# 64x64 array quarters instead of block-diagonal 128x128 operands in the recurrence of block 1

## The chip, the cores and the metric

The kernel runs on one core of a Trainium2 chip. The metric is the device time of one execution in microseconds (us), as a median of several runs; the profile is one further execution, with its own span. The core has a matrix engine (TensorE: PE for its matmuls, PEld for its weight loads), three engines that work on vectors (VectorE: DVE, ScalarE: ACT, GpSimd: POOL) and queues that start DMA transfers (SP is the one that loads weights). Each engine works through its own instructions in order and waits on semaphores for the others.

## What is computed

A chain of layers for 256 tokens of width 1024. Block 1 is an RWKV7 layer with its output projection, a dense feed-forward, an attention layer and a mixture of experts; block 2 is two further transformer layers with a context sequence. Only the RWKV7 recurrence is touched by the change. For each of 16 heads of 64 channels it carries a 64x64 state S over the tokens (wkv7_scan of the reference):

```python
def step(S, inp):
    r_t, w_t, k_t, v_t, a_t, b_t = inp
    sa = jnp.einsum('bhvk,bhk->bhv', S, a_t)
    S = (S * w_t[:, :, None, :] + sa[..., None] * b_t[:, :, None, :]
         + v_t[..., None] * k_t[:, :, None, :])
    return S, jnp.einsum('bhvk,bhk->bhv', S, r_t)
...
y = wkv7_scan(_heads(r), _heads(decay), _heads(k), _heads(v), -kk, kk * a_h)
```

All of it is float32. The rest of the layer, and all else in the program, is the same in both kernels.

## The kernel before

The function wkv does the recurrence in chunks of 64 tokens: four chunks for the 256 tokens, and two heads (a pair, 128 channels) at a time, so that there are eight pairs. Within a chunk the recurrence becomes matrix products of 64x64 blocks and the inverse of a triangular 64x64 matrix. A pair goes through four stages, each a Python generator that yields after each step:

- prep (8 steps): decays, the scaled vectors b and k and the queries, then the pairwise products g1 and g2 within each chunk, masked by VectorE into Aab, Rb, Aak, Rk, and b and k turned token-major (Btok, Ktok).
- invert (17 steps): (I - A)^-1 by merging diagonal blocks from 2 to 64 in five levels. In each level Q is transposed into T, X = mask * (Aab T), Q = Q + X Q.
- walk (14 steps): the four chunks one after another, since each needs the state S of the one before.
- finish (3 steps): group norm, bonus, gate, and the split of the result yT for the output projection.

The two heads of a pair stand side by side on the 128 partitions. To keep them apart in one 128x128 product, the operands are **block-diagonal**: each chunk has 128 columns, of which one 64x64 block belongs to each head and the other two are zero. The buffers bbd, kbd, abd and rbd are zeroed once by GpSimd and only their diagonal blocks are written; the masks have zeros off the blocks. So a tile for one pair is 128x512, a step of invert is four matmuls of 128x128 (function blocks) or four transposes (function transposes), and VectorE masks or adds 128x512 elements.

All products of the recurrence are float32 matmuls. In the trace each stands as two records on PE, each with its own weight load on PEld, and we call such a record a pass; a transpose is one pass.

At most a few pairs are in flight. The list stages gives each stage a start and a length in units of a pair's turn, and the steps of all pairs are sorted by that due time; each engine's instructions then stand about in that order. So prep of one pair, invert of an earlier one and walk of a still earlier one alternate on the engines. Behind every sixth step of wkv (ADA_EVERY = 6) comes one step of another job, ada, which computes block 2's modulation: it loads 1 MB of ada_w (two 512 KB tiles of the six-tile pool wraw, two tiles of which the gate weights hold meanwhile) and does four matmuls with 32 stationary columns and 512 moving columns. These four go to four column groups of the array (written 128*32 in the trace). There are 48 such steps; their DMAs are the only large loads during wkv.

The tiles of the recurrence lie in slots that the projections have left and in five tiles of the pool whl (the names wkvd and wkvx in the rows). When the last pair's result is there, the output projection rwkv_out begins (whi,yTh in the rows).

Of the kernel before, what the change touches and what calls it, by code (L numbers as in the profile page):

```python
# [16 lines left out]
P = 128  # L17
T = 256
# [21 lines left out]
# weight groups held for the last token tile; weights loaded before the lent tiles come in; transposed pairs whose  # L40
# scaling VectorE shares; columns per piece of a weight's split
# [17 lines left out]
def shape_consts():  # L59
    """Masks, permutations and rotary tables: they depend on shapes alone."""  # L60
# [14 lines left out]
    add("bd_strict", same64 & (r < c))  # L75
    add("bd_incl", same64 & (r <= c))
    add("lv0T", ((r // 2) == (c // 2)) & (r < c))
    for lv in range(1, 6):
        b = 2 ** lv
        add(f"lv{lv}", ((r // (2 * b)) == (c // (2 * b))) & ((r // b) % 2 == 1) & ((c // b) % 2 == 0))  # L80
# [39 lines left out]
    groups = {"consts_w": ("bd_strict", "bd_incl", "lv0T", "lv1", "lv2", "lv3", "lv4", "lv5"),  # L120
# [16 lines left out]
def pack(inputs):  # L137
    """Only layout: every vector that goes along partitions is laid out as [128, n]."""
# [20 lines left out]
class Wt:  # L159
    """A weight unit on chip: k-tiles of [128, ncol], as high and low parts."""  # L160
# [16 lines left out]
class Act:  # L177
    """Activations with the contraction on partitions: k-tiles of [128, ntok], high and low parts."""
# [5 lines left out]
class Net:  # L184
    def __init__(self, ctx, tc, a):
# [12 lines left out]
        # tiles that the next weights are loaded into (None: one of their own)  # L198
# [80 lines left out]
    def split(self, hi, lo, src):  # L279
        """src as hi + lo, both readable by the fast float32 matmul."""  # L280
# [3 lines left out]
    def rpow(self, out, x, n, mul, add):  # L284
        """out = (x * mul + add) ** -0.5 for an [128, n] tile."""
# [5 lines left out]
    def wload(self, src, nk, ncol):  # L291
        """Loads [nk*128, ncol] by parts of at most 1024 columns of k-tiles and splits them."""
# [66 lines left out]
    def mmT(self, out, w, x, nk, w0, w1):  # L359
        """out [w1 - w0, 256] = w^T x over nk k-tiles, the weights being the stationary operand."""  # L360
# [6 lines left out]
    def lin_T(self, ch, x, nk, src, n, evac, mcol=P):  # L367
        """Channel-major output: for units of 256 columns evac(c0, ntiles, psum [128, ntiles, 256])."""
# [17 lines left out]
    def to_T(self, ch, src, x, nk=KD, scale=None, bias=None, f32=None):  # L386
        """src(tb) token-major [128, nk*128] -> x (channel-major hi/lo), optionally scaled and shifted per channel."""
# [34 lines left out]
    def layer_norm(self, h, gi, out):  # L422
        """In: h[tb] pre-norm sums [128,1024]; out(tb) normalised, ln_g/ln_b row gi = (layer, which)."""
# [74 lines left out]
    # LoRA hidden states, channel-major: tanh(xw @ w1), xa @ a1, sigmoid(xg @ g1)  # L498
# [42 lines left out]
    # kk = normalised k * k_k per head  # L541
# [36 lines left out]
def wkv(N, st, ch=0):  # L578
# [43 lines left out]
    for x in ("bbd", "kbd", "abd", "rbd"):  # L622
        for t in bufs[x]:
            nc.gpsimd.memset(t, 0.0)
# [1431 lines left out]
```

## Time and profile before

| | |
|---|---|
| median of 3 runs | 2950.31 us (2949.16 to 2954.93) |
| span of the profiled execution | 2942.9 us |
| PE busy | 2824.4 us (96%) |
| PEld busy | 2336.0 us (79%) |
| DVE busy | 2279.5 us (77%) |
| ACT busy | 1809.3 us (61%) |
| mean granted TensorE clock | 0.976 |

The runs' times are 6 to 12 us above the span: they hold what lies around the program's own instructions. In the rows, PE is busy while a matmul is somewhere in the array; matmuls overlap in it, so the busy time of a group is more than its share of the engine, and the time of a steady stream is read from the starts of its records. 128*64 behind the tiles' names is the part of the array that a matmul takes: rows (contraction) times columns (stationary columns). "x8" counts records. The clock is given as a share of full speed, 1.0 for 2.4 GHz and 0.5 for 1.2 GHz.

### The profile page before, as it was taken

The numbers are of one execution on the slowest core, as the hardware profiler recorded it, in microseconds if no ns is written. First come the engines' busy times: TensorE is split into PE (matmuls) and PEld (weight loads), VectorE is DVE, ScalarE is ACT, GpSimd is POOL, SyncE is SP. The second block draws the span as 40 slices with busy tenths as digits, with TensorE's granted clock in tenths as the row PEclk, the third lists the DMA queues.
The fourth block names the chain that finished last, engine by engine and source line by source line (L and its number), as shares of the span: only waits on it lengthen the run. The fifth ranks groups of instructions, "written<-read, shape, count | busy, mean of one in ns | idle before, by whom it ended". The sixth has DMA issues, their size and how long they took to land. (4 is left out here: it accounts for less than half of the span.)

```text
span 2942.9 us, 46516 instructions
## 1 busy us (share of the span) xinstructions
PE 2824.4 (96%) x16596; PEld 2336.0 (79%) x16596; DVE 2279.5 (77%) x4406; ACT 1809.3 (61%) x3665; POOL 70.5 (2%) x96
## 2 busy tenths in 40 slices
PE   8999989999998999999999999979989999989898
PEld 8677779988866777778777777758978799877898
DVE  7455456568578999999999999977686786876767
ACT  5334345444466878787877878756444665666655
POOL 0001110000000000000000000000000000000000
PEclk9899989999999999999999999989989999999999
DMA  7346646654425999999999999965532356521463
GB/s 246 102 153 208 207 163 194 187 157 140 158 90 158 347 346 340 347 361 330 352 355 344 345 346 358 352 236 171 159 111 87 116 180 192 158 94 44 138 190 125
DMA packets 356247, 639.16 MB, mean 217 GB/s; under 512 B 25733, under 2 KB 152965, under 8 KB 356006
## 3 DMA queue, kind: packets, MB, share of 16 engines
q1 hardware_dynamic: 348768, 625.58, 63.2%
q10 hardware_dynamic: 7238, 10.52, 1.1%
q8 instruction: 133, 2.18, 0.3%
q14 instruction: 108, 0.88, 0.1%
HBM read 634.97 MB, written 1.05 MB: 216 GB/s over the span
## 5 line engine op out<-in xcount | busy, mean ns | idle before, releaser
L245 DVE TENSOR_TENSOR wlo<-wraw,whi 128x512 fp32r<-128x512 f32 (+1 forms) x2181 | 1377.4, 683 | 268.1 <-ACT whi L242 207.5
L242 ACT ACTIVATE whi<-wraw 128x512 fp32r<-128x512 f32 (+1 forms) x2181 | 1216.2, 621 | 452.7 <-PE ps L257 340.2
L257 PE MATMUL ps<-whi,xg 128*128 128x512 f32 x1792 | 498.7, 397 | 1.0 <-ACT whi L242 1.0
L257 PEld LDWEIGHTS ps<-whi,xg 128*128 128x128 f32 x1792 | 327.3, 188 | 84.7 <-ACT whi L242 23.6
L257 PE MATMUL ps<-wlo,xg 128*128 128x512 f32 x896 | 295.4, 398 | 0.0
L257 PE MATMUL ps<-whi,hT 128*128 128x512 f32 x896 | 259.9, 401 | 0.0
L257 PE MATMUL ps<-hT0h,whi 128*128 128x256 f32 (+2 forms) x872 | 215.3, 284 | 3.8 <-ACT whi L242 3.3
L257 PE MATMUL ps<-hT0l,whi 128*128 128x256 f32 (+2 forms) x872 | 215.1, 284 | 0.3 <-DVE hT0l L245 0.3
L257 PEld LDWEIGHTS ps<-wlo,xg 128*128 128x128 f32 x896 | 168.1, 188 | 55.7 <-DVE wlo L245 20.2
L257 PE MATMUL ps<-whi,hid 128*128 128x512 f32 x704 | 193.6, 411 | 9.6 <-DVE cv L254 3.7
L257 PEld LDWEIGHTS ps<-whi,hT 128*128 128x128 f32 x896 | 164.3, 188 | 33.3 <-ACT whi L242 0.6
L257 PEld LDWEIGHTS ps<-hT0h,whi 128*128 128x128 f32 (+2 forms) x872 | 167.0, 192 | 4.9 <-ACT whi L242 3.5
L257 PEld LDWEIGHTS ps<-whi,hid 128*128 128x128 f32 x704 | 133.6, 194 | 45.7 <-issue 13.4
L257 PEld LDWEIGHTS ps<-hT0l,whi 128*128 128x128 f32 (+2 forms) x872 | 167.1, 192 | 1.0 <-DVE hT0l L245 0.5
L257 PE MATMUL ps<-wlo,hT 128*128 128x512 f32 x448 | 167.5, 416 | 0.0
L257 PE MATMUL ps<-hT1h,whi 128*128 128x256 f32 (+1 forms) x504 | 127.9, 290 | 21.3 <-ACT whi L242 21.3
L254 DVE SCALAR_TENSOR_TENSOR cv<-ps,vecs,cv 128x255 f32<-128x255 f32 x264 | 124.6, 478 | 14.1 <-ACT cv L242 12.6
L257 PE MATMUL ps<-hT1l,whi 128*128 128x256 f32 (+1 forms) x504 | 125.9, 286 | 0.2 <-DVE hT1l L245 0.2
L257 PE MATMUL ps<-hT0h,wlo 128*128 128x256 f32 (+2 forms) x872 | 124.1, 283 | 1.6 <-DVE wlo L245 1.5
L257 PEld LDWEIGHTS ps<-hT0h,wlo 128*128 128x128 f32 (+2 forms) x872 | 112.8, 191 | 3.0 <-DVE wlo L245 2.6
L257 PEld LDWEIGHTS ps<-hT1h,whi 128*128 128x128 f32 (+1 forms) x504 | 96.3, 191 | 23.6 <-ACT whi L242 21.7
L257 PEld LDWEIGHTS ps<-wlo,hT 128*128 128x128 f32 x448 | 84.2, 188 | 28.4 <-DVE wlo L245 10.4
(539 smaller groups left out, 4708.6 us busy)
## 6 DMA issues: line engine op xcount, KB each, us to landing
wraw<-moe_w_down SPq DMA_DIRECT2D x224, 512.0 KB, 5.5
wraw<-moe_w_gate SPq DMA_DIRECT2D x222, 512.0 KB, 5.1
wraw<-moe_w_up SPq DMA_DIRECT2D x222, 512.0 KB, 5.5
wraw<-ffn_w_up SPq DMA_DIRECT2D x154, 512.0 KB, 4.0
wraw<-ada_w SPq DMA_DIRECT2D x96, 512.0 KB, 4.0
wraw<-ffn_w_down SPq DMA_DIRECT2D x88, 512.0 KB, 3.7
wraw<-ev_w_in SPq DMA_DIRECT2D x56, 512.0 KB, 3.7
wraw<-rwkv_w_rkv SPq DMA_DIRECT2D x24, 512.0 KB, 6.6
```

Of the source, the lines that this page charges most:

```text
L242: self.nc.scalar.activation(out, in_, f, **kw)
L245: (eng or self.nc.vector).tensor_tensor(out, x, y, op=op)
L254: (eng or self.nc.vector).scalar_tensor_tensor(out, x, s, y, op0=op0, op1=op1)
L257: self.nc.tensor.matmul(out, l, r, start=start, stop=stop)
```

## The change

The block-diagonal operands go. Each product of the recurrence is now two matmuls of 64 rows by 64 columns, one for each head: the first head on partitions 0 to 63 in and out, the second on 64 to 127. A tile for one pair is 128x256 (four chunks of 64 columns; the head is the partition half). Only AR, which holds a and r side by side, keeps 128 columns for each chunk. What follows from that in the code:

- blocks issues eight matmuls instead of four, walk's new helper both issues two instead of one; the moving operand is 64 columns (128 for g1 and g2, as before).
- transposes becomes flip: the transpose mode is replaced by an ordinary float32 matmul with a 64x64 identity, eight for each tile.
- invert no longer transposes Q in each level. It transposes once at the start, and then T is carried along: T = T + (X Q)^T is one more call of blocks and one more VectorE addition in each of the first four levels. Its steps fall from 16 to 12 in the list stages.
- abd and rbd, and the four ACT copies into them for each pair, are gone: walk reads a and r from AR, which has three buffers instead of one. The memsets are gone.
- VectorE's masks and additions work on 128x256 instead of 128x512.
- The five tiles of whl and the slots 6 and 12 are no longer used by wkv.
- ADA_EVERY is 5 instead of 6, for there are 304 steps of wkv instead of 336.

```diff
-ADA_EVERY = 6
+ADA_EVERY = 5
...
-WKV_BUFS = dict(abd=3, rbd=3, Aak=3, Rb=3, Rk=3, Btok=3, Ktok=3, Q=3, Aab=2, T=2, X=2, bbd=1, kbd=1, AR=1)
+WKV_BUFS = dict(Aak=3, Rb=3, Rk=3, Btok=3, Ktok=3, Q=3, Aab=2, T=2, X=2, bb=1, kb=1)
...
-    def blocks(ps, l, r):
+    def blocks(ps, l, r, w=64):
         for n in range(4):
-            s = slice(n * P, (n + 1) * P)
-            N.mm(ps[:, s], l[:, s], r[:, s], True, True)
+            for q in heads:
+                N.mm(ps[q, n * w:(n + 1) * w], l[q, n * 64:(n + 1) * 64], r[q, n * w:(n + 1) * w], True, True)
-    def transposes(dst, src, ch=ch):
-        pt = N.ps(ch)
+    def flip(ps, l):
         for n in range(4):
-            N.tr(pt[:, n * P:(n + 1) * P], src[:, n * P:(n + 1) * P])
-        N.act(dst, pt)
+            for q in heads:
+                N.mm(ps[q, n * 64:(n + 1) * 64], l[q, n * 64:(n + 1) * 64], N.ident[q, q], True, True)
...
-        for h in range(2):
-            q = slice(h * 64, h * 64 + 64)
-            N.tt(half(bbd)[q, :, h, :], c4(bv)[q], c4(di)[q], ALU.mult)
-            N.tt(half(kbd)[q, :, h, :], c4(k2)[q], c4(di)[q], ALU.mult)
+        N.tt(bb, bv, di, ALU.mult)
+        N.tt(kb, k2, di, ALU.mult)
...
     def invert(pr, levels):
...
+        pt = N.ps(ch)
+        flip(pt, Q)
+        N.act(Ti, pt[:, 0:T])
+        yield
         for lv in levels:
-            transposes(Ti, Q)
-            yield
             px = N.ps(ch)
             blocks(px, Aab, Ti)
...
             pq = N.ps(ch)
             blocks(pq, X, Q)
-            N.tt(Q, Q, pq, ALU.add)
+            if lv != levels[-1]:
+                blocks(pq[:, T:2 * T], Q, X)
+            N.tt(Q, Q, pq[:, 0:T], ALU.add)
+            if lv != levels[-1]:
+                N.tt(Ti, Ti, pq[:, T:2 * T], ALU.add)
             yield
...
+        def both(out, l, r, start, stop):
+            for q in heads:
+                N.mm(out[q], l[q], r[q], start, stop)
```

How the change stands in PE's order is shown at two places. The first is a stretch in the middle, with invert of one pair and walk of another; in the names, ps<-wkvx (of before) and ps<-wkvd_1064 (of after) are Aab T, ps<-wkvd_1066,wkvx and ps<-wkvd_1063,wkvd_1064 are X Q, ps<-wkvd_1064,wkvd_1063 is the new product for T, VS, ru and S are walk's operands, and wraw,silu_c is ada. Before:

```order
L257 MATMUL ps<-lora_hid,wkvw 128x128 x2
L257 MATMUL ps<-wraw,silu_c 32x512 x4
L257 MATMUL ps<-wkvd_1066,wkvx 128x128 x8
L257 MATMUL ps<-VS,wkvd_1062 128x64
L257 MATMUL ps<-wraw,silu_c 32x512 x4
L257 MATMUL ps<-rk_ind,wkvw 128x2 x2
L257 MATMUL ps<-ru,wkvd_1066 128x64
L277 MATMUL ps<-ident,wkvd_1066 128x128 x4
```

After, on the same engine and at the same point of the same pair's prep (the two matmuls lora_hid,wkvw):

```order
L261 MATMUL ps<-lora_hid,wkvw 128x128 x2
L261 MATMUL ps<-wkvd_1063,wkvd_1064 64x64 x8
L261 MATMUL ps<-wkvd_1064 64x64 x8
L261 MATMUL ps<-wraw,silu_c 32x512 x4
L261 MATMUL ps<-VS,wkvd_1061 64x64 x2
L261 MATMUL ps<-rk_ind,wkvw 128x2 x2
L261 MATMUL ps<-wkvd_1063,wkvd_1064 64x64 x8
L261 MATMUL ps<-wkvd_1064,wkvd_1063 64x64 x8
```

Each group of the recurrence has twice the matmuls, the transposes of Q have gone, and the product for T has come in behind X Q.

The second place is the end of wkv on PE: the last matmuls of ada. Before:

```order
L257 MATMUL ps<-wraw,silu_c 32x512
L257 MATMUL ps<-wkvx 128x128 x4
L257 MATMUL ps<-ru,wkvd_1063 128x64
L257 MATMUL ps<-wraw,silu_c 32x512 x3
L257 MATMUL ps<-VS,wkvd_1065 128x64
L257 MATMUL ps<-wkvd_1066,wkvx 128x128 x4
L277 MATMUL ps<-ident,adar 128x128 x4
L257 MATMUL ps<-lora_hid,g2a 128x256
```

After:

```order
L261 MATMUL ps<-wraw,silu_c 32x512 x2
L261 MATMUL ps<-VS,wkvd_1061 64x64 x2
L261 MATMUL ps<-S_3872,wkvd_1061 64x64 x2
L261 MATMUL ps<-wkvd_1063,wkvd_1064 64x64 x7
L261 MATMUL ps<-ru,wkvd_1063 64x64 x2
L261 MATMUL ps<-wkvd_1063,wkvd_1064 64x64
L261 MATMUL ps<-wkvd_1064,wkvd_1063 64x64 x8
L261 MATMUL ps<-VS,wkvd_1063 64x64 x2
L261 MATMUL ps<-ru,wkvd_1062 64x64 x2
L281 MATMUL ps<-ident,adar 128x128 x4
```

Before, the last group of ada stands beside the last level of the last pair's inversion; now it stands in the middle of that inversion, with two and a half levels still to come.

## Rows read from the trace of the kernel before

**Rows 1.** Windows: busy us (records) by engine, granted clock, DMA share, GB/s.
```profile
121.00:382.00 261.00, 261.00 (x1924) 186.88 (x1922) 139.46 (x335) 88.63 (x244) 23.28 (x34) 0.99 0.58 193
382.00:406.00 24.00, 16.16 (x82) 13.44 (x79) 10.10 (x33) 8.86 (x24) 5.03 (x7) 0.67 0.61 208
```

**Rows 2.** Groups by form on PE, 121 to 406 us: xcount, busy, mean ns, idle.
```profile
L257 PE MATMUL ps<-wkvx 128*128 128x128 f32 x444 | 62.9, 284 | 0.0
L257 PE MATMUL ps<-wkvd,wkvx 128*128 128x128 f32 x320 | 44.0, 281 | 0.0
L257 PE MATMUL ps<-ru,wkvd 128*128 128x64 f32 x176 | 35.6, 286 | 0.9 <-DVE ru L756 0.6 <-ACT ru L242 0.3
...
L277 PE MATMUL ps<-ident,wkvx 128*128 128x128 f32 x64 | 8.9, 274 | 0.0
```

**Rows 3.** Timeline of weight loads, 232.2 to 233.4 us: start, length, xcount.
```profile
232.14 0.30 PEld L257 LDWEIGHTS ps<-VS,wkvd 128*128 128x128 f32 x2 [0.84 <-issue]
232.36 0.30 PEld L257 LDWEIGHTS ps<-S,wkvd 128*128 128x128 f32 x2
232.58 0.97 PEld L257 LDWEIGHTS ps<-wkvd,wkvx 128*128 128x128 f32 x8
```

**Rows 4.** Timeline of PE where parts of the array alternate (attention of later layers).
```profile
822.68 0.93 PE L257 MATMUL ps<-kTm,qT 64*128 64x128 f32 x8
...
824.50 0.92 PE L257 MATMUL ps<-kTm,qT 64*128 64x128 f32 x4
...
2649.30 0.66 PE L257 MATMUL ps<-R,mlav 128*64 128x128 f32 x8
2649.78 0.61 PE L257 MATMUL ps<-R,mlavc 128*64 128x128 f32 x8
```

**Rows 5.** Group by form on PEld, 2640 to 2705 us: loads of 64 columns.
```profile
L257 PEld LDWEIGHTS ps<-R,mlav 128*64 128x64 f32 x114 | 6.0, 136 | 5.3 <-ACT S L242 3.3 <-issue 1.7 <-ACT R L242 0.3
```

**Rows 6.** Timeline of PE into and out of one group of ada.
```profile
235.70 0.28 PE L257 MATMUL ps<-wkvx 128*128 128x128 f32 x1
235.91 0.62 PE L257 MATMUL ps<-wraw,silu_c 128*32 128x512 f32 x2
...
236.38 0.59 PE L257 MATMUL ps<-wraw,silu_c 128*32 128x512 f32 x1
236.90 0.32 PE L257 MATMUL ps<-VS,wkvd 128*128 128x64 f32 x1
```

**Rows 7.** Groups by form on DVE, 121 to 406 us: 512 and 256 columns.
```profile
L245 DVE TENSOR_TENSOR wkvx<-ps,lora_hid 128x512 f32<-128x512 f32 x48 | 33.0, 690 | 47.6 <-PE ps L257 47.0
...
L245 DVE TENSOR_TENSOR gy<-gy,ps 128x256 f32<-128x256 f32 x14 | 5.8, 415 | 1.1 <-ACT gy L242 1.0
```

**Rows 8.** Timeline of one link of walk's chain: PE, DVE, PE.
```profile
384.41 0.43 PE L257 MATMUL ps<-ru,wkvd 128*128 128x64 f32 x2
...
384.97 0.21 DVE L756 COPY ru<-ps 128x64 f32<-128x64 f32 x1
...
385.40 0.43 PE L257 MATMUL ps<-ru,wkvd 128*128 128x64 f32 x2
```

**Rows 9.** Timeline of weight loads in the tail of wkv, 391.8 to 392.9 us.
```profile
391.89 0.55 PEld L257 LDWEIGHTS ps<-S,wkvd 128*128 128x128 f32 x2
392.31 0.55 PEld L257 LDWEIGHTS ps<-ru,wkvd 128*128 128x128 f32 x2
```

**Rows 10.** Timeline of PE around the end of wkv.
```profile
381.26 1.06 PE L257 MATMUL ps<-wraw,silu_c 128*32 128x512 f32 x6
...
399.79 0.69 PE L257 MATMUL ps<-ru,wkvd 128*128 128x64 f32 x2 [0.32 <-DVE ru L756]
...
405.98 1.11 PE L277 MATMUL ps<-ident,yz 128*128 128x128 f32 x4 [5.50 <-POOL yz L245]
```

**Rows 11.** Windows as in rows 1: half-array matmuls among others; a full DMA stretch.
```profile
820.00:885.00 65.00, 60.00 (x344) 41.46 (x343) 48.72 (x161) 47.26 (x150) 0.00 (x0) 0.97 0.22 74
...
1500.00:1505.00 5.00, 5.00 (x24) 4.04 (x23) 4.63 (x9) 4.06 (x8) 0.00 (x0) 1.00 0.97 353
```

More of the change, by code (lines that the diff above doesn't have):

```diff
@@ L599, in wkv @@
     nc.scalar.dma_start(g2b[:32], a["rwkv_gate_g2"][0][P:160])
-    room = []
-    for i in (1, 2, 3, 5, 6, 12):
-        t = N.slot(i, f"wkvd{i}")
-        room += [t[:, j * 512:(j + 1) * 512] for j in range(4)]
-    for i in range(WKV_EXTRA):
-        t = N.whl.tile([P, 1024], F32, name="wkvx", tag=("whi", "wlo")[i % 2])
-        room += [t[:, j * 512:(j + 1) * 512] for j in range(2)]
+    wide = [N.slot(i, f"wkvd{i}") for i in (1, 2, 3, 5)]
+    room = [t[:, j * 512:(j + 1) * 512] for t in wide for j in range(4)]
     wk = N.slot(13, "wkvw")
-    bufs = {n: [room.pop(0) for _ in range(k)] for n, k in WKV_BUFS.items()}
+    bufs = {"AR": [room.pop(0) for _ in range(WKV_AR)]}
+    room = [t[:, j * 256:(j + 1) * 256] for t in room for j in range(2)]
+    bufs.update((n, [room.pop(0) for _ in range(k)]) for n, k in WKV_BUFS.items())
     def buf(name, pr):
@@ L683, in prep @@
         N.tt(arv[:, :, 1, :], c4(rT[:, cs]), Dx[:, :, 1:65], ALU.mult)
-        for h in range(2):
-            q = slice(h * 64, h * 64 + 64)
-            N.tt(half(bbd)[q, :, h, :], c4(bv)[q], c4(di)[q], ALU.mult)
-            N.tt(half(kbd)[q, :, h, :], c4(k2)[q], c4(di)[q], ALU.mult)
+        N.tt(bb, bv, di, ALU.mult)
+        N.tt(kb, k2, di, ALU.mult)
         yield
         g1 = N.ps(WKV_PC[0])
-        blocks(g1, bbd, AR)
+        blocks(g1, bb, AR, P)
         def msk(out, g, part, m):
-            src = bc(half(g)[:, :, part, :], 2, 2)
-            mk = bc(c[m].rearrange("p (h t) -> p h t", h=2), 1, 4)
-            N.tt(half(out), src, mk, ALU.mult)
-        msk(buf("Aab", pr), g1, 0, "bd_strict")
-        msk(buf("Rb", pr), g1, 1, "bd_incl")
+            N.tt(c4(out), half(g)[:, :, part, :], bc(c[m], 1, 4), ALU.mult)
+        msk(buf("Aab", pr), g1, 0, "h_strict")
+        msk(buf("Rb", pr), g1, 1, "h_incl")
         yield
         g2 = N.ps(WKV_PC[0])
-        blocks(g2, kbd, AR)
-        msk(buf("Aak", pr), g2, 0, "bd_strict")
-        msk(buf("Rk", pr), g2, 1, "bd_incl")
-        for h in range(2):
-            q = slice(h * 64, h * 64 + 64)
-            N.act(half(buf("abd", pr))[q, :, h, :], arv[q, :, 0, :])
-            N.act(half(buf("rbd", pr))[q, :, h, :], arv[q, :, 1, :])
-        yield
-        transposes(buf("Btok", pr), bbd)
-        transposes(buf("Ktok", pr), kbd)
+        blocks(g2, kb, AR, P)
+        msk(buf("Aak", pr), g2, 0, "h_strict")
+        msk(buf("Rk", pr), g2, 1, "h_incl")
+        yield
+        pt = N.ps(WKV_PC[0])
+        flip(pt[:, 0:T], bb)
+        flip(pt[:, T:2 * T], kb)
+        N.act(buf("Btok", pr), pt[:, 0:T])
+        N.act(buf("Ktok", pr), pt[:, T:2 * T])
         yield
@@ L739, in walk @@
                 N.act(vs4[h * 64:h * 64 + 64, :, cp, :], src)
-        Aak, Rb, Rk, Q, abd, rbd = (buf(x, pr) for x in ("Aak", "Rb", "Rk", "Q", "abd", "rbd"))
+        Aak, Rb, Rk, Q, AR = (buf(x, pr) for x in ("Aak", "Rb", "Rk", "Q", "AR"))
         Kt, Bt, fac = buf("Ktok", pr), buf("Btok", pr), st["fac", pr]
+        def both(out, l, r, start, stop):
+            for q in heads:
+                N.mm(out[q], l[q], r[q], start, stop)
         S0 = None
@@ L745, in walk @@
         for n in range(4):
-            s = slice(n * P, (n + 1) * P)
-            vn = VS[:, n * 64:(n + 1) * 64]
+            s = slice(n * 64, (n + 1) * 64)
+            av, rv = half(AR)[:, n, 0, :], half(AR)[:, n, 1, :]
+            vn = VS[:, s]
             o = n * 128
-            N.mm(pw[:, o:o + 64], Aak[:, s], vn, True, n == 0)
+            both(pw[:, o:o + 64], Aak[:, s], vn, True, n == 0)
             if n:
-                N.mm(pw[:, o:o + 64], abd[:, s], S0, False, True)
+                both(pw[:, o:o + 64], av, S0, False, True)
             RU = N.smp.tile([P, 128], F32, name="ru", tag="ru", bufs=2)
@@ L769, in walk @@
             yo = py[:, n * 64:(n + 1) * 64]
-            N.mm(yo, Rk[:, s], vn, True, False)
+            both(yo, Rk[:, s], vn, True, False)
             if n:
-                N.mm(yo, rbd[:, s], S0, False, False)
-            N.mm(yo, Rb[:, s], U, False, True)
+                both(yo, rv, S0, False, False)
+            both(yo, Rb[:, s], U, False, True)
             if n < 3:
@@ L817, in finish @@
         yield
-    stages = ((finish, 2, 3.3, 0.6), (walk, 13, *WKV_T[0]), (lambda pr: invert(pr, (1, 2, 3, 4, 5)), 16, *WKV_T[1]), (prep, 7, *WKV_T[2]))
+    stages = ((finish, 2, 3.3, 0.6), (walk, 13, *WKV_T[0]), (lambda pr: invert(pr, (1, 2, 3, 4, 5)), 12, *WKV_T[1]), (prep, 7, *WKV_T[2]))
     order = []
```

34 lines of the change are left out of this document (17 added, 17 removed).

## The prediction, made before the changed kernel ran

> **What bounds the kernel now.** I read the windows first, then the groups of the stretch that the change touches, then its timeline. In the windows [rows 1] the reader is to see that PE is busy for all of 121 to 382 us, at full clock, while DVE is busy 139 of the 261 us and ACT 89. This is wkv from the first to the last matmul of ada. Busy PE alone proves little, since overlapping matmuls count as busy; so I read the pace. Weight loads of 128 columns start 0.11 us apart without a break, over eight in a row and over pairs [rows 3], whether the moving operand has 128 columns (wkvd,wkvx) or 64 (VS, S). So a pass costs 0.111 us: the stream of 128 columns takes that, and where only 64 stream, the load does. The seven groups of the recurrence that pass through PE hold 1436 records (the first has 444, the last 64) [rows 2]; the program has 1440 passes. 1440 x 0.111 = 160 us of the 261 plus 24. The idle column of these groups is below 1 us each: PE waits for nobody, others wait for PE (VectorE's masks waited 47 us for it [rows 7]). What is taken off PE here comes off the time, until something else is late.
>
> Behind it lies a tail, 382 to 406 us [rows 1]: the last pair's walk and finish, PE busy 16 of 24 us by this count and the clock down to 0.67. It is a chain of waits, not PE's work: the last transposes, at 405.98, waited 5.50 us for GpSimd's group norm [rows 10].
>
> **The change part by part.**
>
> *PE's passes.* Before, a pair has 104 matmuls or transposes, in 180 passes. Now it has 208 matmuls of one quarter, each two passes: 416, or 3328 for eight pairs. If the two heads' quarters run side by side, that is 1664 pair-passes. The trace shows no two diagonal quarters at once, but it shows both halves of the idea [rows 4]. With 64 rows: four records of kTm,qT on one half take 0.92 us, and eight that alternate between the halves take 0.93. With 64 columns: eight records of R,mlav, alternating, start and are followed by the next eight 0.48 us later, 0.06 us a record, though each streams 128 columns, which alone takes 0.111. So I take the side-by-side pace. A quarter's load has 64 columns: such a load is 0.136 us long [rows 5], and one of 128 columns 0.30 - 0.11 = 0.19 [rows 3], so 64 columns less save about 0.055. Stream and load are thus both half of 0.111; with a little on top I take 0.057 us for a pair-pass of 64 columns. g1 and g2 still stream 128 columns: 128 pair-passes at 0.111 = 14.2 us; the other 1536 at 0.057 = 87.6. Sum 102 us against 160: **58 us less PE**. That invert now does a product for T instead of transposing is in the count.
>
> *Switches.* When PE goes from one array shape to another the overlap of load and stream is lost: into ada 0.21 us pass between starts where 0.11 is normal, out of it 0.52 where a stream of 512 columns at 0.111 for 128 takes 0.44 [rows 6]; 0.08 to 0.10 us each way, and I take 0.10. Counting shapes in PE's order, wkv has 169 switches before and 213 after (prep's and finish's 128-wide matmuls now stand between quarters): 44 x 0.10 = 4.4 us more.
>
> *VectorE and ACT.* For each pair, 16 operations of 512 columns at 0.69 and four of 256 (on half the partitions) at 0.42 become 22 of 256 columns at 0.42 [rows 7]: 12.7 to 9.2 us, 27 us less in all. ACT loses four full evacuations and the copies to abd and rbd. All this lay beside PE and is worth nothing by itself; but DVE's 139 us become 112 in a stretch of about 210, the same share as before, so it does not become the bound.
>
> *ada.* Its 48 steps and 384 records stay. In 210 us its 48 MB are some 230 GB/s, where another stretch moved 353 [rows 11]. Four free tiles hold two steps' loads. I cost it at nothing but jitter, in the next term; if each step waited 1 us for its load, that would be 48 us, so it is not harmless, but the pace of loads leaves room.
>
> *Waits inside the stretch.* PE's groups get half as long while a hand-over stays: from the start of two matmuls to VectorE's copy 0.56 us, and 0.22 from its end to the next matmul [rows 8]. With three pairs interleaved most is covered, as before, where PE lost almost nothing. I allow 9 us, between 0 (as before) and 30 (a second rival).
>
> *Sum for 121 to 382.* Passes in this part before: 160 less 6 in the tail (some 28 matmuls) = 154. After: 102 less 9 (150 quarter matmuls stand behind ada's last group) = 93. 261 - 154 + 93 + 4 + 9 = 213 us.
>
> *The tail.* ada now ends earlier in the order, with two and a half levels of the last inversion still to come and nothing to fill the gaps. A level is X (0.46 PE, 0.34 to DVE, 0.42, 0.22 back) and Q with T (0.92, 0.34, 0.42, 0.22): 3.3 us, so about 8 us, of which 2 stood there before. Against it, at the low clock passes start 0.21 us apart [rows 9], twice 0.111, and a chunk of walk has 14 of them; at half of this a chunk loses 1.4 us, about 3.5 for the two and a half that ran cold. 24 + 6 - 3.5 = 27 us.
>
> So wkv's end moves from 121 + 261 + 24 = 406 to 121 + 213 + 27 = 361 us: **45 us earlier**. What follows it stands in the same order, and waits for the last yT as before. The span of 2942.9 would be 2898; the median lies 7.4 us above the span, and 2950.3 - 45 is 2905.
>
> **The rivals.**
>
> *The two quarters do not run side by side (slower).* Both heads write the same PSUM bank, on different partitions, from different row halves. In the trace the row halves that overlap (kTm,qT) write different banks, and the column parts that share a bank (R,mlav) use all rows; the two together are not shown. Nor is the rate: the densest stream in the rows starts a record every 0.06 us, and this needs one every 0.028. If records go one at a time, at 0.057, the sum is 3072 x 0.057 + 256 x 0.111 = 204 us instead of 102: 261 - 154 + (204 - 17) + 4 + 2 = 300, with a tail of 30: 451 against 406, so 2995. The point from which it decides: at 0.046 us a record the gain is gone. For it speaks only that no row shows the case; against it that each half of the array works by itself in both directions.
>
> The Trainium skill states a rule for it: in TensorEngine Tiling (Array Packing), under Restrictions and Gotchas, different row tiles cannot access one PSUM bank at the same time. By that rule the sum would be the 204 us just named. No run here shows it either way, as the rows for row halves have separate banks.
>
> *The chain becomes the bound (smaller gain).* A pair's turn falls from some 33 us to 26. walk is a chain of four chunks with three or four links of 0.8 us and a state update each, about 13 us: 41% of a turn before, half of one now, and each link also queues behind other pairs' work on DVE. If turns cannot fall below 30 us, eight turns give back 30 us: 2935, with values to 2950. For it: the handed-over pieces are shorter, and the hand-over is not. Against: DVE's load falls by the same share as PE's.
>
> *The clock falls in the stretch (slower).* Quarters fill half of the array. If half of the 213 us ran at half clock, that is some 100 us more: 3005. Against: in a stretch with half-array matmuls among others the granted clock was 0.97 [rows 11], and in the stretch at hand ada still fills the array every few us.
>
> **How the numbers follow.** Forecast 0.64, chain-bound 0.19, serial quarters 0.13, clock 0.04. The forecast's own range is 2885 (no stalls at all, pair-pass at 0.055, a shorter tail) to 2928 (30 us less of gain than passes and switches give). About 0.2%, 6 us, is what a measurement of this kernel can tell from none. The forecast is all faster; of the chain's 0.19, 0.12 is faster and 0.07 the same; the other two are slower. That gives 0.76, 0.07, 0.17. A range of 2885 to 2955 leaves out the two slow cases and a little below: 0.19.
>
> **What would show it.** Right: records of the recurrence in 64*64 form, about 3328, that start in pairs some 0.01 us apart and 0.057 us from pair to pair; the first rwkv_out matmul near 361 us; DVE's 256-column operations at 0.42; the clock at 1.0 until about 330 us. A start every 0.05 us or more means the first rival. Pairs at 0.057 with PE's groups ended by DVE and ACT mean the second. A wait of the ada matmuls for wraw means that I undercosted the loads. What would make it wrong altogether is a change outside wkv: what comes behind the recurrence should stand as before, only earlier.

## The result and the profile after

The changed kernel takes **2909.08 us** (median of four runs, 2905.18 to 2911.15) against 2952.62 us of the kernel before beside it (2949.16 to 2955.71): a ratio of **0.9856, 95% interval 0.984 to 0.9872**. Run again later as an experiment of its own it took 2905.64 us, ratio 0.9853 (0.9832 to 0.9874). So 43 to 44 us are gone, 1.5%. The prediction was 2905 us.

The windows of the changed kernel, which answer to [rows 1], with the same columns: from the first to the last matmul of ada, and from there to the output projection's first matmul.

```profile
121.00:335.00 214.00, 212.91 (x3544) 135.62 (x3544) 106.92 (x337) 52.80 (x175) 23.31 (x34) 0.99 0.73 237
335.00:368.00 33.00, 23.68 (x345) 17.36 (x341) 14.95 (x50) 11.25 (x32) 4.97 (x7) 0.74 0.44 145
```

The stretch in which PE is busy throughout has shrunk from 261 to 214 us, at the same clock; the tail behind it has grown from 25 to 33.

The groups by form on PE, 100 to 400 us (xcount, busy, mean ns of one, idle before and its releasers), which answer to [rows 2]:

```profile
L261 PE MATMUL ps<-wraw,silu_c 128*32 128x512 f32 x384 | 76.2, 614 | 0.9 <-DMA wraw<-ada_w 0.9
L261 PE MATMUL ps<-wkvd,wkvd 64*64 64x64 f32 x1152 | 44.3, 220 | 0.7 <-DVE wkvd L249 0.7
L261 PE MATMUL ps<-VS,wkvd 64*64 64x64 f32 x352 | 29.7, 236 | 0.5 <-DVE S L253 0.3
L261 PE MATMUL ps<-ru,wkvd 64*64 64x64 f32 x352 | 29.4, 237 | 1.5 <-DVE ru L762 1.1 <-ACT ru L246 0.3
L261 PE MATMUL ps<-wkvd 64*64 64x64 f32 x640 | 28.4, 220 | 0.1
L261 PE MATMUL ps<-wkvd,wkvd 64*64 64x128 f32 x256 | 23.1, 291 | 0.6 <-DVE wkvd L249 0.6
L261 PE MATMUL ps<-ident,wkvd 64*64 64x64 f32 x384 | 15.4, 221 | 0.0
L261 PE MATMUL ps<-S,wkvd 64*64 64x64 f32 x192 | 15.0, 228 | 0.0
```

The seven 64*64 groups hold 1152 + 352 + 352 + 640 + 256 + 384 + 192 = 3328 records. Whether they run side by side is read from the pace. The timeline around 227 us (start, length, engine, names, count), full clock:

```profile
226.04 1.01 PEld L261 LDWEIGHTS ps<-ident,wkvd 64*64 64x64 f32 x32 [0.84 <-PE ps L261]
226.96 0.55 PEld L261 LDWEIGHTS ps<-wkvd 64*64 64x64 f32 x16
227.43 0.55 PEld L261 LDWEIGHTS ps<-ident,wkvd 64*64 64x64 f32 x16
```

The 32 loads at 226.04 are followed by the next group 0.92 us later, and the 16 at 226.96 by theirs 0.47 us later: **0.029 us a record, 0.058 us a pair**. Read one by one, the loads of the two heads start 0.007 us apart, and the next pair 0.058 us later. In [rows 3] a record took 0.11 us. The record's own length, 0.22 us, says nothing of this; only starts do.

The output projection's first matmul (whi,yTh) stands at 367.88 us, where the kernel before has it at 406.7: 39 us earlier in these two profiles, and 40.5 us in the second profile of the changed kernel, where it stands at 366.2. All that follows is the same program, but not always in the same time: from that matmul to the end of the span it takes 2536.2 us in the profile of the kernel before and 2539.9 and 2537.6 us in the two of the changed kernel. The last section deals with this.

### The profile page after: what moved, and what is told of

Read it like the earlier page. It is cut to its first block, busy times and chain, and to the rows that moved or that the text cites. A ratio compares the mean times of both kernels' runs of the same rounds, so it can differ in the third digit from the quotient of the medians.

```text
span 2907.8 us, 50259 instructions
## 1 busy us (share of the span) xinstructions
PE 2786.7 (96%) x18484; PEld 2290.5 (79%) x18484; DVE 2252.5 (77%) x4422; ACT 1776.7 (61%) x3601; POOL 66.2 (2%) x88
```

## The experiments

Theory: the recurrence was bound by TensorE's passes, and quarters that run side by side took half of them away. Rivals: the quarters overlap only by some accident of the order; or the gain is that of the shorter chain (the inversion's transpose was dropped in four of five levels as part of the same change) or of VectorE's shorter operations; and, for what was missing to the forecast, the tail.

### The heads not next to each other in the program

```diff
-        for n in range(4):
-            for q in heads:
+        for q in heads:
+            for n in range(4):
                 N.mm(ps[q, n * w:(n + 1) * w], l[q, ...], r[q, ...], True, True)
```

(the same in flip.)

> The changed kernel with the loops of its two helpers turned round: the four chunks of head 0 first, then the four chunks of head 1, where the changed kernel takes the two heads of a chunk by turns. The arithmetic, the engines' other work and the number of records stay the same; only the recurrence's walk still has the heads next to each other. Theory A (each diagonal quarter takes its records from a line of its own, so that the heads run side by side even when four instructions lie between them): the time of the changed kernel, 2909 us, within 6 us; in the trace the two halves' records still alternate. Theory B (what runs side by side is only an instruction and its neighbour in program order, by a pair of neighbours): the 1216 pairs of records outside the walk become single ones of 0.057 us each, about 69 us more, 2975 us, and the trace shows four chunks of head 0 with nothing beside them.

Measured: 2930.28 us, ratio 0.9937 (0.9914 to 0.9959), some 23 us more than the changed kernel; the first output projection matmul is 22.6 us later, at 390.5. Neither theory holds: about a third of the 69 us is lost. The weight loads show why. In the timeline of this kernel, the same kinds of groups as above (32 records, of which 30 stand in the first row, and 16):

```profile
235.94 1.28 PEld L261 LDWEIGHTS ps<-ident,wkvd 64*64 64x64 f32 x30 [0.84 <-PE ps L261]
...
250.80 0.82 PEld L261 LDWEIGHTS ps<-wkvd,wkvd 64*64 64x64 f32 x16
...
257.47 0.76 PEld L261 LDWEIGHTS ps<-wkvd,wkvd 64*64 64x64 f32 x16 [0.84 <-issue]
```

Sixteen loads take 0.76 to 0.82 us, where the changed kernel has 0.55, and where sixteen one after the other would take 15 x 0.058 + 0.136 = 1.0 (the last one's own length is 0.136). Read one by one, the sixteen at 250.80 are two rows of eight: in each row the loads start 0.058 us apart, and the second row begins 0.287 us behind the first, together with the first row's sixth load. So a quarter alone takes a record every 0.058 us, and in a group that stands by itself three of eight pairs overlap. Where groups follow each other without a break, as at 235.94, a new row of eight begins every 0.287 us, 0.036 us a record: the end of one row overlaps the beginning of the next. In these groups the second head's records thus begin no earlier than with the sixth of the eight records that stand ahead of them in the program. That the two heads alternate in the program is part of the gain.

### One product issued twice

```diff
             blocks(px, Aab, Ti)
+            blocks(px, Aab, Ti)
```

> The changed kernel with the first product of each level of the inversion issued twice into the same bank: 320 more matmuls, 640 more records, 320 pairs of records. Nothing else of the program changes and the result is the same. Theory A (the recurrence is still bound by TensorE's instructions): 320 x 0.058 us = 18.6 us more, of which what fell into TensorE's idle time is saved, so +13 to +19 us, 2922 to 2928 us. Theory B (the chain of matmul, eviction and next matmul inside a pair is now the bound): the copy adds only 8 x 2 x 0.029 = 0.46 us to each of 40 levels where the chain passes, and three pairs are in flight, so about 18.6 / 3 = 6 us more at most, 2909 to 2915 us.

Measured: 2919.57 us, ratio 0.9898 (0.9882 to 0.9915), 12 to 13 us above the changed kernel's 0.9853 to 0.9856; the first output projection matmul is at 376.7, 9 to 10.5 us later than in the changed kernel's two profiles. This is between the theories, much nearer to A: 10 to 13 of 18.6 us are paid. The starts of PE's records tell where the rest is. From the start of each record to the start of the next, the quarter records take 17.6 to 18.1 us more than in the changed kernel's two profiles, nearly all of the 18.6. What is saved is saved in ada, here in its group from 100 to 400 us:

```profile
L261 PE MATMUL ps<-wraw,silu_c 128*32 128x512 f32 x384 | 67.4, 612 | 2.0 <-DMA wraw<-ada_w 2.0
```

The same 384 records take 67.4 us of PE instead of 76.2, though they wait for their loads no less (2.0 us of idle time against 0.9). They stand in fewer groups. Two places of the changed kernel's timeline, each with what follows it:

```profile
230.15 1.06 PE L261 MATMUL ps<-wraw,silu_c 128*32 128x512 f32 x8
231.15 0.27 PE L261 MATMUL ps<-VS,wkvd 64*64 64x64 f32 x2
...
333.41 1.05 PE L261 MATMUL ps<-wraw,silu_c 128*32 128x512 f32 x2
334.38 0.33 PE L261 MATMUL ps<-VS,wkvd 64*64 64x64 f32 x4
```

Eight records in a row (four matmuls) take 1.00 us until the next record starts, two (one matmul) 0.97: ada's four matmuls lie on four column groups of the array and run side by side, so a group costs about 1 us however many of the four stand in it. In the changed kernel's order on PE the 48 steps of ada are split into 67 groups, in this kernel's order into 61. So TensorE is still what sets the time here, and no gaps are needed to explain what is missing.

### VectorE's mask done twice, and the transpose made anew

```diff
             N.tt(c4(X), c4(px[:, 0:T]), bc(c[f"lv{lv}"], 1, 4), ALU.mult)
+            N.tt(c4(X), c4(px[:, 0:T]), bc(c[f"lv{lv}"], 1, 4), ALU.mult)
```

> The changed kernel with VectorE's masking of each level's first product done twice: 40 more VectorE instructions of 256 columns with about 0.42 us each, 16.8 us of VectorE's time in all, in the chain of the inversion. Theory A (TensorE is still the bound in the recurrence, the chain has slack): 0 to +4 us, 2909 to 2913 us, and what there is comes from the last pairs, where there is nothing beside the chain: 10 instructions x 0.42 us = 4 us. Theory B (the chain or VectorE is the bound): 17 us more where the turns of the pairs don't overlap, at least 17 / 2 = 8 us more where two pairs share it, 2917 to 2926 us.

Measured: 2904.95 us, ratio 0.9842 (0.9825 to 0.986): no more than the changed kernel. The windows 121 to 334 us, first of the changed kernel, then of this one:

```profile
121.00:334.00 213.00, 211.91 (x3534) 135.17 (x3532) 106.92 (x337) 52.80 (x175) 23.31 (x34) 0.99 0.73 238
```

```profile
121.00:334.00 213.00, 212.31 (x3609) 138.27 (x3607) 121.37 (x377) 55.15 (x181) 23.50 (x34) 0.99 0.73 240
```

VectorE is busy 14 us longer, and PE is no further behind (it has even got 75 records further; ada stands in 64 groups here, not in 67). Without ada, all that PE does until the output projection takes 176.5 us by the starts, 2 us more than in the changed kernel, and that lies in the tail, as theory A has it. The second test on the chain puts the transpose back:

```diff
             blocks(pq, X, Q)
-            if lv != levels[-1]:
-                blocks(pq[:, T:2 * T], Q, X)
             N.tt(Q, Q, pq[:, 0:T], ALU.add)
-            if lv != levels[-1]:
-                N.tt(Ti, Ti, pq[:, T:2 * T], ALU.add)
             yield
+            if lv != levels[-1]:
+                pt = N.ps(ch)
+                flip(pt, Q)
+                N.act(Ti, pt[:, 0:T])
+                yield
```

(16 steps for the inversion, ADA_EVERY = 6.)

> The changed kernel with the inversion's transpose made anew in each level, as the kernel before did, by eight matmuls against the identity and a ScalarE copy, instead of being carried by eight matmuls and a VectorE addition; one step more in each of four levels, so 16 steps for the inversion, and the weight pipeline's step comes at every sixth step as before. TensorE's record count is the same; four additions per pair leave VectorE (32 x 0.42 = 13 us in all) and four copies come to ScalarE; the chain of each level grows by one matmul group and one eviction, about 1.5 us, 6 us a pair. Theory A (TensorE is the bound): 0 to +5 us, 2909 to 2914 us, with +4 to +6 us in the last pair alone, where the chain has nothing beside it. Theory B (the chain is the bound): 6 us in each of 8 turns, up to +48 us, 2930 to 2957 us.

Measured: 2903.69 us, ratio 0.9841 (0.9814 to 0.9869). The chain of each inversion is longer by four links, and the time is not. So the carried T gains nothing here; theory A holds in both. The first output projection matmul even came 8.2 us earlier than in the first profile of the changed kernel (6.4 earlier than in the second), at 359.7: ada's last group stands at 339.6, and the tail behind it is 20 us. 3 to 5 us of this are ada's, which stands in 61 groups. The end of the span is earlier by 3.9 us only.

### The carried transpose alone, in the kernel before

```diff
+        transposes(Ti, Q)
+        yield
         for lv in levels:
-            transposes(Ti, Q)
-            yield
             ...
             blocks(pq, X, Q)
+            if lv != levels[-1]:
+                pt = N.ps(ch)
+                blocks(pt, Q, X)
             N.tt(Q, Q, pq, ALU.add)
+            if lv != levels[-1]:
+                N.tt(Ti, Ti, pt, ALU.add)
```

(12 steps for the inversion, ADA_EVERY = 5.)

> The kernel before with one part of the change alone: the inversion carries T and Q side by side (four 128x128 block-diagonal matmuls and an addition in place of four transposes and a ScalarE copy in four of the five levels), 12 steps instead of 16 and the weight pipeline at every fifth step; the array is used as before, with 128x128 operands. TensorE gets 16 transposes of one record less and 16 matmuls of two records more per pair, 128 records of 0.111 us = 14 us more. Theory A (TensorE is the bound, and the gain of the change is that of the quarters): 2950 + 5 to 14 = 2955 to 2964 us, ratio 1.002 to 1.005. Theory B (the chain within a pair is what the change shortened, by about 1.5 us in each of four levels and 8 pairs = 48 us): faster than before by 10 us or more, 2900 to 2940 us.

Measured: 2957.4 us, ratio 1.003 (1.0019 to 1.0041): 9 us slower than before, inside theory A's 5 to 14. Passes are what is paid for, in the kernel before too: by the starts, the recurrence's records take 15.8 us more until the output projection, and ada 9 us less, in 59 groups instead of 70. So the carried transpose is no part of the gain. The change's other parts (shorter VectorE operations, fewer ScalarE copies, no memsets) were not taken out one by one; that 14 us more of VectorE cost nothing speaks against a gain from the first of these.

### Three tries at the tail

The weight pipeline's pace, and the planner's numbers for the stages:

```diff
-ADA_EVERY = 5
+ADA_EVERY = 6
```

> The changed kernel with one step of the weight pipeline at every sixth step of the recurrence, as before, instead of every fifth: the 48 steps then reach to step 291 of 304 instead of 243, into the tail, where the changed kernel has only the last pairs' chains. Theory A (the tail of 32 us has 9 us of idle TensorE and a fallen clock, and the weights' matmuls waited 4.4 us for their loads because they come closer together): 3 to 10 us less until the output projection's first matmul, 2898 to 2905 us. Theory B (what is in the tail is the chain, and each weight step in between delays it by its 1.2 us): 0 to +4 us, 2908 to 2912 us.

Measured: 2906.73 us, ratio 0.986 (0.9837 to 0.9883), the same; the first output projection matmul at 366.7 us. Theory B. Windows of this kernel: the tail as a whole, and five microseconds of it; then, from its timeline of PE, two of the groups there:

```profile
335.00:367.00 32.00, 26.38 (x228) 10.46 (x228) 8.42 (x32) 7.67 (x23) 4.47 (x6) 1.00 0.86 306
```

```profile
355.00:360.00 5.00, 3.96 (x26) 0.96 (x22) 0.81 (x3) 1.31 (x5) 0.57 (x1) 1.00 1.02 403
```

```profile
358.84 1.05 PE L261 MATMUL ps<-wraw,silu_c 128*32 128x512 f32 x4 [0.40 <-DMA wraw<-ada_w]
360.12 1.05 PE L261 MATMUL ps<-wraw,silu_c 128*32 128x512 f32 x4 [0.23 <-DMA wraw<-ada_w]
```

In the tail ada now fills the chain's gaps: without ada, all that PE does until the output projection takes 165.0 us by the starts, 9 to 10 less than in the changed kernel. But ada itself takes 79.1 us instead of 70 to 72. It stands in 71 groups instead of 67, and in the tail the steps follow each other so fast that ada comes as quickly as its loads do (the DMA engines full, 403 GB/s, in the five microseconds shown). The one pays for the other. The clock is at 1.00 throughout this tail, and that brings nothing either.

```diff
-WKV_T = ((2.3, 1.0), (0.6, 1.7), (0.0, 1.0))
+WKV_T = ((1.9, 1.0), (0.6, 1.3), (0.0, 1.0))
-    stages = ((finish, 2, 3.3, 0.6), ...
+    stages = ((finish, 2, 2.9, 0.6), ...
```

> The changed kernel with its three planner numbers for the stages changed: the inversion is spread over 1.3 turns instead of 1.7, walk and finish begin 0.4 turns earlier. The work is the same; in the program's order a pair is done 0.4 turns earlier, so ramp and tail are 0.4 of a turn shorter. A turn is about 213 / 8 = 27 us of TensorE work. Theory A (TensorE is the bound in the steady part, so the chain may be tighter): the 12 steps of the last inversion come in shorter distance and the tail loses part of its idle 9 us: 2 to 8 us less, 2899 to 2905 us. Theory B (the chain of the inversion is near its bound already, three products of one level in 1.7 turns): with the tighter order TensorE waits for the evictions: +3 to +10 us, 2910 to 2917 us.

Measured: 2914.37 us, ratio 0.9881 (0.9864 to 0.9897), 7 to 9 us slower than the changed kernel, which is theory B by the time. The waits of PEld for VectorE's part of the inversion, 121 to 371 us (total, times, longest), first in the changed kernel, then in this one:

```profile
PEld ps L261 <- DVE wkvd L249: 7.5, 9, 0.8
```

```profile
PEld ps L261 <- DVE wkvd L249: 11.2, 16, 1.0
```

The waits are longer by 3.7 us, but the first output projection matmul stands at 370.6, only 2.7 to 4.4 us later than in the changed kernel, and without ada (72.7 us) all that PE does until then takes 175.2 us by the starts, as in the changed kernel (174.4 to 174.8). Where the rest of the 7 to 9 us lies is not shown.

With both edits together:

> The changed kernel with both of these: the weight pipeline at every sixth step, and the inversion over 1.3 turns with the walk 0.4 turns earlier. If both gain by filling the tail, the gains don't add up in full: 5 to 12 us less than the changed kernel, 2895 to 2902 us. If the tail is the chain alone, no less than the better of the two single ones, 2904 to 2912 us.

Measured: 2916.92 us, ratio 0.9885 (0.9869 to 0.9902): no better than the shorter inversion alone. Ada is split into 78 groups here and takes 86.7 us.

The third try fills the idle array of the last pair's walk with products that nobody reads.

```diff
+    def fill(pr, l, r, k=1):
+        if pr == 7:
+            pd = N.ps(ch)
+            for _ in range(k):
+                blocks(pd, l, r)
             N.act(RU[:, 0:64], pw[:, o:o + 64])
+            fill(pr, Kt, Q)
             nc.vector.tensor_copy(RU[:, 64:128], pw[:, o + 64:o + 128])
+            fill(pr, Kt, Q)
             if n < 3:
                 S0 = Sn
+            fill(pr, Kt, Q, 1 if n < 3 else 10)
```

> The changed kernel with idle TensorE time of the last pair's walk filled by matmuls whose results nobody reads: one group of eight 64x64 matmuls (16 records, 0.46 us) after each of the walk's 12 product groups, while the chain waits for the eviction, and ten groups (4.6 us) after the last, while the group norm of that pair runs on the other engines. All 21 groups are 9.7 us of records at full clock. In the changed kernel the granted clock is 0.50 to 0.58 from 350 to 370 us, with TensorE busy for 4.17 of 5 us and less in the records. Theory A (the slow records of the tail are the clock's doing, and work in its gaps holds it at 1.0): the rows from 350 to 370 us show the clock near 1.0, the walk of the last pair gets shorter than 13.7 us in spite of the added work, and the projection behind it begins with a full clock: 2 to 6 us less, 2903 to 2907 us. Theory B (the chain's evictions on ScalarE and VectorE set the tail's length and the clock is only a consequence): 0 to +5 us, since a group of 0.46 us now stands ahead of each matmul of the chain, 2909 to 2914 us.

> The changed kernel itself, unaltered, beside the one with the filled tail and the same runs of the kernel before: both theories expect 2909 us, ratio 0.984 to 0.987. It gives the middle to which the small differences of the experiments are held.

Measured: 2908.29 us filled, ratio 0.9852 (0.9832 to 0.9871), and 2905.64 us unaltered, 0.9853 (0.9832 to 0.9874): the same. The clock did what theory A says, and the time what theory B says. Windows 350 to 370 us, of the changed kernel and of the filled one:

```profile
350.00:370.00 20.00, 12.09 (x95) 8.78 (x94) 6.00 (x22) 5.97 (x19) 3.81 (x6) 0.52 0.28 106
```

```profile
350.00:370.00 20.00, 20.00 (x332) 17.12 (x333) 10.09 (x29) 10.23 (x27) 3.29 (x5) 1.00 0.37 133
```

The first output projection matmul stands at 361.9 us in the filled kernel and at 366.2 in the unaltered one beside it. But ada's last group was already 2.1 us earlier in the filled one, before any filling begins, so the fill bought 2.2 us in the tail, not more. At full clock the tail is still 361.9 - 331.4 = 30.5 us: the clock is a small part of its length. (The fill also stands in the chain, up to 0.46 us ahead of a product, so a full clock alone might be worth a little more.) And the span's end is 4.8 us later than in the unaltered kernel's profile, which the last section deals with.

The last run puts the transpose made anew and the fill together.

> The changed kernel with the two edits put together that brought the output projection forward in the trace: the inversion's transpose made anew in each level with the weight pipeline at every sixth step (its first output projection matmul stood 8.2 us earlier), and the 21 idle groups of eight matmuls in the last pair's walk (6.0 us earlier). Theory A (the tail's clock and its filling are worth their time to the end): ratio 0.978 to 0.982, 2886 to 2898 us, with the first output projection matmul at 352 to 358 us. Theory B (what is won in the recurrence is taken back further on, where the granted clock of one stretch behind the experts, the same instructions in each kernel, lies at 0.5 for more or less of its time from profile to profile): the first output projection matmul earlier by 8 to 14 us, the whole 2900 to 2909 us.

Measured: 2902.44 us, ratio 0.9838 (0.9823 to 0.9853), with the first output projection matmul at 362.1 us: not the sum of the two. The whole lies in theory B's range, but its reason is not shown here: that matmul came 4 to 6 us earlier than in the changed kernel, not 8 to 14. It is the lowest median here, but its interval overlaps that of the changed kernel; no run shows a version that certainly beats it.

## Why the prediction came out

**What bounds it: right.** Passes on PE. With one product issued twice the quarter records take 17.6 to 18.1 us more, of 18.6, while more work for VectorE and a longer chain cost nothing, and carrying the transpose gave nothing.

**PE's passes: right.** 3328 records, as counted, at 0.058 us a pair where 0.057 was taken from loads and streams of 64 columns. **Switches: right in size.** Starts out of ada into quarters are 0.530 us apart (60 cases from 121 to 334 us; 0.52 before [rows 6]), and starts from a quarter into ada mostly 0.15, where 0.03 is normal.

**VectorE: right.** The groups by form on DVE, 121 to 335 us, answer to [rows 7]:

```profile
L249 DVE TENSOR_TENSOR wkvd<-ps,lora_hid 128x256 f32<-128x256 f32 x70 | 27.8, 421 | 37.6 <-PE ps L261 37.2
L249 DVE TENSOR_TENSOR wkvd<-wkvd,ps 128x256 f32<-128x256 f32 x67 | 25.7, 418 | 21.3 <-PE ps L261 21.3
```

0.42 us each, and VectorE still waits for PE, not the other way.

**Stalls and ada: the sum right, the split not.** The stretch took 214 us where 213 was reckoned. Of the 9 us of stalls some 8 are there: 2642 starts between quarter records of 64 columns add up to 84.1 us, 0.032 each instead of 0.029. But ada's loads, costed at nothing but jitter, are late as well. The waits of PEld from 121 to 335 us:

```profile
PEld ps L261 <- DMA wraw<-ada_w: 4.4, 7, 1.1
```

In the kernel before, the group of ada's loads shows 0.3 us of this. The prediction had named this wait as the sign that the loads were undercosted; it is 4.4 us (2.6 in the second profile), not the 48 of its bad case. By the starts ada takes 71.7 us, and 70.7 in the kernel before, since it stands in 67 groups now and stood in 70.

**The tail: the term that failed.** It was put at 27 us, from ada's end to the last yz transposes, and is 32 (335.2, where ada's last record starts, to 367.11). The timeline of PE there:

```profile
346.11 0.68 PE L261 MATMUL ps<-wkvd,wkvd 64*64 64x64 f32 x16 [0.68 <-DVE wkvd L249]
...
351.20 0.69 PE L281 MATMUL ps<-ident,yz 128*128 128x128 f32 x2 [1.17 <-POOL yz L249]
...
352.23 0.69 PE L281 MATMUL ps<-ident,yz 128*128 128x128 f32 x2
352.71 1.06 PE L261 MATMUL ps<-lora_hid,g2a 128*128 128x256 f32 x2
...
354.32 1.22 PE L261 MATMUL ps<-lora_hid,g2b 32*128 32x256 f32 x2
...
361.12 0.48 PE L261 MATMUL ps<-ru,wkvd 64*64 64x64 f32 x4 [0.40 <-DVE ru L762]
367.11 1.11 PE L281 MATMUL ps<-ident,yz 128*128 128x128 f32 x4 [5.51 <-POOL yz L249]
367.88 0.78 PE L261 MATMUL ps<-whi,yTh 128*128 128x512 f32 x1
```

The pairs are numbered 0 to 7. From ada's end at 335.2 to the end of the last product of pair 7's inversion (346.11 plus 0.68) 11.6 us pass, where 8 were reckoned from its own links: steps of pair 6 and the finish of pair 5 stand between them in PE's order, and 1.2 us of pair 6's finish behind them. The walk of pair 7 runs from 347.97 to 361.60, 13.6 us, against 16.1 of the kernel before (384.4 to 400.5 [rows 8, 10]); so 2.4 us are won where 3.5 were reckoned. In the middle of it stand the transposes of pair 6, which waited for GpSimd, and g2a and g2b of pair 7's own finish, which do not need the walk. They stood there in the kernel before as well, but mostly before the clock fell (at 390.2 us there, at 350.8 here):

```profile
388.55 0.66 PE L277 MATMUL ps<-ident,yz 128*128 128x128 f32 x4 [1.24 <-POOL yz L245]
389.04 0.60 PE L257 MATMUL ps<-lora_hid,g2a 128*128 128x256 f32 x2
...
389.74 0.83 PE L257 MATMUL ps<-lora_hid,g2b 32*128 32x256 f32 x2
```

Their lengths add up to 2.1 us, and now to 0.69 + 0.69 + 1.06 + 1.22 = 3.7. The last 5.5 us, a wait for GpSimd, are those of [rows 10]. 11.6 + 1.2 + 13.6 + 5.5 = 32. The walk and the rest of the inversion were reckoned as if the last pair were alone on PE. Filling the tail left it at 30 us, and moving ada into it or starting the walk earlier won nothing.

**From span to median: a wrong reading, and luck.** The prediction, and the section on the time before, read the distance between the span of 2942.9 and the runs' times as what lies around the program. It isn't: in every run with both numbers the time is 1.7 to 1.9 us above that run's own span (2909.56 and 2907.8; 2952.12 and 2950.3 of the kernel before). So the profiled execution of the kernel before was itself near 2944.7 us, 5.6 below the median of 2950.3. The forecast took 45 us from that median. In the profiles wkv won 39 to 40.5, and the spans differ by 35.1 and 39.1; the medians differ by 43.5 and 44.4. No run shows where the medians' 3 to 5 us beyond wkv's gain come from, as the kernel before has a single profile, of a fast execution. That 2905 came within 4 us, with the tail 5 us too short, is partly luck.

**The rivals.** Quarters one after the other: no, by the pace of 0.029 us a record; that overlap undone in part costs 23 us. Both heads of a product write one PSUM tile, on different partitions, at that pace. The rule of the Trainium skill (TensorEngine Tiling (Array Packing), Restrictions and Gotchas), that different row tiles cannot access one PSUM bank at the same time, would have doubled the 0.058 us a pair; for two diagonal quarters this case's trace does not agree with it. The chain as the bound: not in the steady stretch, as the longer chain at no cost shows. Squeezed into 1.3 turns, the inversion cost 7 to 9 us in the median, of which its profile shows 3 to 4 before the output projection and none in the recurrence's own records, so this run doesn't tell how far the chain is from being the bound. The clock: at 0.99 in the stretch; no.

## What to carry to other kernels

Two products of half the array's width and half its height each, on diagonal quarters, can replace one block-diagonal product of the whole array at half its time, if the stream of columns halves with it and the two stand next to each other in the program; grouped by quarter instead, a third of the overlap's worth was lost here. When PE is the bound, count its records and read their starts; as long as a product issued twice costs its full time, shorter links and lighter vector work gain nothing. Matmuls on different column groups of the array belong next to each other: each group that a step is split into costs as much as the whole step. Reckon a tail with all that stands in the same engine's order between its links, and take a run's own span to compare it with its time.

## What the runs showed beside this

**What the splitting of ada costs.** By the starts of PE's records, from ada's first matmul to the output projection's first (us):

| kernel | all | ada | groups of ada | all but ada |
|---|---|---|---|---|
| before | 285.1 | 70.7 | 70 | 214.4 |
| changed, two profiles | 246.5, 244.6 | 71.7, 70.2 | 67 | 174.8, 174.4 |
| heads not next to each other | 267.1 | 67.0 | 67 | 200.1 |
| one product twice | 255.6 | 63.5 | 61 | 192.1 |
| mask twice | 243.9 | 67.4 | 64 | 176.5 |
| transpose made anew | 238.2 | 67.1 | 61 | 171.1 |
| carried transpose, kernel before | 292.4 | 61.8 | 59 | 230.6 |
| ada at every sixth step | 244.1 | 79.1 | 71 | 165.0 |
| shorter inversion | 247.9 | 72.7 | 67 | 175.2 |

A group is what stands in a row of ada's records in PE's order. Most of the edits also moved the places where ada's four matmuls stand apart. The change itself is hardly touched by this (70 groups before, 67 after), but differences of a few us between the experiments are. In the changed kernel the median group of two, four, six or eight records takes 0.98, 0.98, 0.99 or 1.00 us. With each of the 48 steps in one piece, 19 groups less at 0.99 us would be some 19 us less; this is an estimate from these rows and was not tried.

**A stretch far behind the change whose clock differs from profile to profile.** Between two marks in block 2's first layer (the last ktok transpose and the last matmul of rpb) PE is never idle in these profiles and does the same work in every kernel (the last of the three windows takes in four records more at its ends). Windows of that stretch: the changed kernel, the changed kernel again, and the one with the filled tail.

```profile
2169.00:2203.00 34.00, 34.00 (x279) 32.71 (x277) 20.09 (x41) 11.21 (x22) 0.00 (x0) 1.00 0.36 113
```

```profile
2160.50:2199.00 38.50, 38.50 (x279) 37.17 (x277) 20.76 (x42) 11.15 (x21) 0.00 (x0) 0.87 0.32 107
```

```profile
2159.00:2204.00 45.00, 45.00 (x283) 43.18 (x281) 21.03 (x42) 11.24 (x21) 0.00 (x0) 0.73 0.30 92
```

34, 38.5 and 45 us for the same instructions, at clocks of 1.00, 0.87 and 0.73, the first two of one and the same program. Just before it, the changed kernel's first profile had a low clock and rose; in the other two it was at full clock there and fell within the stretch:

```profile
2155.00:2160.00 5.00, 3.19 (x7) 1.82 (x6) 4.60 (x8) 2.41 (x4) 0.00 (x0) 0.50 0.00 0
```

```profile
2150.00:2155.00 5.00, 3.05 (x12) 2.21 (x13) 3.02 (x5) 1.91 (x4) 1.74 (x1) 0.94 0.36 105
2155.00:2160.00 5.00, 3.73 (x23) 2.85 (x22) 4.70 (x7) 2.56 (x5) 0.27 (x1) 1.00 0.32 94
2160.00:2165.00 5.00, 5.00 (x23) 4.04 (x23) 2.71 (x6) 0.68 (x2) 0.00 (x0) 0.59 0.38 116
```

The first fence is the changed kernel, the second the one with the filled tail. From the output projection's first matmul to the end of the span the filled kernel takes 2546.7 us and the one with the transpose made anew 2544.2, 9.1 and 6.6 more than the changed kernel's second profile; 6.2 and 3.2 of this lie in this stretch. So what they won in the recurrence was gone at the end of their profiles. What decides at which point the clock falls was not tried. It means that a difference of 4 to 11 us between the ends of two single profiles of this kernel says nothing about an edit; the medians do, and the first output projection matmul to within the 1.7 us by which it differs in two profiles of one program.

**Quarters look ahead in the program only a little.** With the heads by turns all pairs overlap (0.029 us a record). With the heads eight records apart three of eight pairs do (sixteen loads in 0.76 to 0.82 us instead of 0.55), and an unbroken run of groups takes 0.036 us a record.
